# The branch gates of a hybrid decoder layer: from eight block products to seven, two of them beside the attention's tail

## The chip, the cores and the metric

The kernel runs on one core of one Trainium2 chip. The metric is the device time of one execution in microseconds. Three executions of the kernel before took 2147.61, 2152.07 and 2151.1 us, median 2151.1 us. A profile of one further execution stands beside them.

The core has five engines with a queue each, which work through their own queue in order and wait for one another by semaphores: TensorE (PE in the profile, with PEld for the loads of its stationary operand), VectorE (DVE), ScalarE (ACT), GpSimd (POOL) and SyncE (SP), which here issues every DMA. Tiles lie in SBUF, with 128 partitions; TensorE writes to PSUM, of which this kernel uses eight banks of 128 x 512 float32.

## The reference

One layer over 1024 tokens with a model width of 2048, in float32:

```python
h = rmsnorm(x, g_pre)
u = h @ w_in
gq, gk, gv, g_gate, g_lr, sq, sk, sv, s_gate = split(u)
o_gla = gla_chunked(gq, gk, gv, log_sigmoid(g_lr @ w_a2 + b_a) / 16)   # 4 heads
o_gla = rmsnorm(o_gla, g_gla_head) * silu(g_gate)
o_sb = stick_breaking(sq, sk, sv) * silu(s_gate)                       # 8 heads
mix = concat(o_gla, o_sb) @ w_out
h = x + rmsnorm(mix, g_post)
out = h + sigmoid(h @ w_ple_gate + b_ple_gate) * (p @ w_ple_proj)
```

The change concerns `g_gate` and `s_gate`, the two branch gates. Each is 1024 columns of `w_in`, so together they are one product of the 1024 x 2048 matrix `h` with a 2048 x 2048 matrix, followed by silu and a multiplication with the attention's output.

## The kernel before

**Layout.** Everything is kept transposed: a tile has 128 features in its partitions and 512 tokens (one half of the sequence, `hf` 0 or 1) in its free dimension. The input `x`, times `g_pre`, lies in `x_act[hf][k]` for the whole projection, 16 blocks of 128 features for each half. The factor of the RMSNorm, `rstd[hf]`, is applied to a result, not to the input.

**Precision.** A float32 operand is held as two tiles, a rounded high part (ScalarE, L104) and the rest as a low part (VectorE, L105). A block product is then three matmuls of 128 x 128 by 128 x 512 into one PSUM bank: high by high, low by high, high by low (L94 is the helper that records every matmul).

**Weights.** There are two kinds of weight tiles. `wload` (L112) brings 128 x 512 (`raw`, `hi`, `lo`) from a pool `w`. `wload2` and `wsplit` (L764, L769) bring 128 x 1024 (`wr` with four buffers, `wh` and `wl` with three) from a pool `mix`, which is opened after the projection has ended. `ar` (three buffers) stages other 128 x 1024 tiles from DRAM in the later part.

**Stages.** `dense` (L135) computes one unit, 128 output columns for both halves, over 16 blocks: 96 matmuls. Units 0 to 39 are the heads' keys, queries and values. Beside them runs the attention: generators in a queue `jobs`, of which `step()` (L156), called once in each of the 16 blocks, advances one at a set rate. So the order of the work is written out by hand as a sequence, with matmuls of the projection and pieces of the attention interleaved. A scheduler at compile time then orders each engine's instructions by this sequence, by raised priorities (`high_priority`: weight loads 700 ahead, evacuations 300 ahead) and by when its own model has their operands and tile buffers ready. A tile's buffer comes back when its last reader is done.

Units 40 to 55 are the branch gates. The first four (`early_gate`, L684) run while the attention still works on its last head; their 128 x 512 tiles come from the attention's ring `u` of twelve buffers. The next ten (`evac_gate`, L702) follow in a pool `gates`. A gate's evacuation multiplies the result with `rstd`, takes a sigmoid, multiplies with the attention's output read back from `o_d`, and stores to `og_d`. The last two units ("late solo", L891 to L917) run in the pool `mix` with wide tiles, one half after the other, beside jobs that read `og_d` back and form sums.

After that the kernel multiplies with `w_out` and with `w_ple_gate`. Both of these 1024 x 2048 by 2048 x 2048 products are already made of seven block products instead of eight (the Strassen-Winograd form): `A11`, `A12`, `A22` and the combinations `S1` to `S4` on one side, and weight blocks combined to `T1` to `T4` on the other. `product` (L777) is one of them for 128 output columns and 512 tokens: 8 blocks, 24 matmuls. `t2_d` and `t3_d` hold combined weights in DRAM for later stages, `fill` (L803) makes a set of eight operands from DRAM, and `st_u` and `st_v` (`u(j)`, `v(j)`) hold running sums in the buffers of the first half's `x_act`.

The PSUM banks are four for results (`dn`), two for `z`, and one each for `t` and `o`.

## Time and profile before

| quantity | value |
|---|---|
| median of three executions | 2151.1 us |
| profiled execution | 2153.95 us, span from first to last instruction 2151.8 us |
| TensorE busy | 2115.5 us, 98% of the span, 9904 matmuls |
| VectorE busy | 1374.1 us, 64% |
| ScalarE busy | 831.0 us, 39% |
| DMA | 300.38 MB, 140 GB/s over the span |

"Busy" is the union of the times in which an engine had an instruction in hand. Matmuls overlap, so the time that a matmul adds is their spacing. In the rows by line, "out<-in" names the tiles written and read, then come the shape, the count, the total and mean time, and the idle time just before with what ended it. In rows of stretches stand each engine's busy time and instruction count, the clock granted to TensorE as a share of full speed, the share of time the DMA engines were busy, and the bytes they moved. The share over the whole span hides that stages differ: DMA moves 54 to 120 GB/s during the attention and 176 to 329 GB/s in the slices behind the wide gates, up to the last but one.

### The profile page before, as it was taken

The page shows a single profiled execution, that of the slowest core. Times are in us where ns is not written, and L with a number is a line of the kernel's source. Part 1 is how long each engine was busy: PE and PEld are TensorE (multiplying, and loading weights), DVE is VectorE, ACT ScalarE, POOL GpSimd, SP SyncE. Part 2 cuts the span into 40 slices and gives each one's busy share as a digit, 9 for nine tenths or more (in the row PEclk, how much of TensorE's full clock was granted, in tenths as well). Part 3 has the DMA queues.
Part 4 walks back from the last instruction along what each step waited for, and adds up shares of the span by engine and source line. Part 5 has one row for each costly group of instructions (what it writes and reads, how often), then busy time and mean ns, then how long its engine had stood idle before and what let it go on. Part 6 is the DMA issues. An engine that isn't in the chain of part 4 may idle for free.

```text
span 2151.8 us, 26865 instructions
## 1 busy us (share of the span) xinstructions
PE 2115.5 (98%) x9904; PEld 1747.3 (81%) x9904; DVE 1374.1 (64%) x2147; ACT 831.0 (39%) x1347; POOL 106.4 (5%) x228
## 2 busy tenths in 40 slices
PE   9999999999999999999999999979999999999998
PEld 6788888888888888888888888868788888778887
DVE  8557676766666666666666232336687787885665
ACT  7333333333455454544544111123233344322332
POOL 3000000000101110110110000000000000000000
PEclk9999999999999999999999999989999999999999
DMA  6222222222233333333344333258787686786763
GB/s 205 73 54 56 59 61 59 55 59 58 62 86 86 75 85 91 85 85 76 93 101 120 93 98 98 87 176 314 291 329 255 207 302 210 265 289 225 232 206 122
DMA packets 215843, 300.38 MB, mean 140 GB/s; under 512 B 122912, under 2 KB 127904, under 8 KB 215712
## 3 DMA queue, kind: packets, MB, share of 16 engines
q1 hardware_dynamic: 215712, 298.67, 45.0%
q8 instruction: 77, 1.26, 0.2%
q14 instruction: 54, 0.44, 0.1%
HBM read 215.25 MB, written 56.10 MB: 126 GB/s over the span
## 4 chain that ended last, share of the span: by engine, by line
PE 82%; DMA 8%; DVE 6%; issue 2%; ACT 1%; SPq 1%; DVEq 0%; ACTq 0%
PE dn L94 72%; PE z L94 6%; PE t L94 2%; PE o L94 2%; DMA wr<-w_g 2%; DVE wl L105 1%; DMA ar<-og_d 1%; DMA xraw<-xT 1%; DMA ar<-h_d 1%; DVE al L105 1%; DMA wr<-w_out 1%; DMA ar<-c_d 0%; DMA ar<-xT 0%; DMA t_d<-wr 0%; DVE wr L759 0%
## 5 line engine op out<-in xcount | busy, mean ns | idle before, releaser
L94 PE MATMUL dn<-ah,hi 128*128 128x512 f32 x1728 | 686.9, 397 | 0.2 <-ACT u L666 0.2
L94 PE MATMUL dn<-al,hi 128*128 128x512 f32 x1728 | 675.4, 391 | 0.9 <-DVE al L230 0.9
L94 PE MATMUL dn<-ah,lo 128*128 128x512 f32 x1728 | 674.3, 390 | 0.0
L94 PE MATMUL dn<-ah,wh 128*128 128x512 f32 x960 | 375.4, 391 | 11.2 <-ACT wh L104 11.2
L94 PEld LDWEIGHTS dn<-al,hi 128*128 128x128 f32 x1728 | 324.3, 188 | 73.0 <-DVE al L230 2.3
L94 PEld LDWEIGHTS dn<-ah,hi 128*128 128x128 f32 x1728 | 324.8, 188 | 72.2 <-issue 2.8
L94 PE MATMUL dn<-ah,wl 128*128 128x512 f32 x960 | 375.7, 392 | 4.6 <-DVE wl L105 4.6
L94 PE MATMUL dn<-al,wh 128*128 128x512 f32 x960 | 374.5, 390 | 0.5 <-DVE al L105 0.5
L94 PEld LDWEIGHTS dn<-ah,lo 128*128 128x128 f32 x1728 | 325.0, 188 | 61.1
L104 ACT ACTIVATE hi<-raw 128x512 fp32r<-128x512 f32 x216 | 135.5, 628 | 300.6 <-PE dn L94 298.7
L105 DVE TENSOR_TENSOR lo<-raw,hi 128x512 fp32r<-128x512 f32 x216 | 150.3, 697 | 151.1 <-ACT hi L104 150.5
L94 PEld LDWEIGHTS dn<-ah,wh 128*128 128x128 f32 x960 | 181.3, 189 | 49.7 <-ACT wh L104 11.6
L94 PEld LDWEIGHTS dn<-ah,wl 128*128 128x128 f32 x960 | 181.6, 189 | 43.3 <-DVE wl L105 5.5
L94 PEld LDWEIGHTS dn<-al,wh 128*128 128x128 f32 x960 | 181.2, 189 | 38.6 <-DVE al L105 1.0
L104 ACT ACTIVATE wh<-wr 128x1024 fp32r<-128x1024 f32 x120 | 126.1, 1056 | 200.0 <-PE dn L94 125.3
L105 DVE TENSOR_TENSOR wl<-wr,wh 128x1024 fp32r<-128x1024 f32 x120 | 146.0, 1219 | 23.4 <-ACT wh L104 22.6
L309 ACT ACTIVATE X<-E 128x256 uint16<-128x256 uint16 (+2 forms) x96 | 81.0, 844 | 136.2 <-DVE E L582 123.2
L577 DVE TENSOR_TENSOR_SCAN X<-X 128x128 f32<-128x128 f32 (+2 forms) x96 | 98.3, 1024 | 36.8 <-POOL X L571 24.4
L592 DVE COPY v<-E 128x512 uint16<-128x512 uint16 (+1 forms) x160 | 63.6, 429 | 67.1 <-DMA E<-X 58.0
L104 ACT ACTIVATE ah<-ar 128x1024 fp32r<-128x1024 f32 x48 | 50.9, 1061 | 100.6 <-DVE ar L762 48.5
L105 DVE TENSOR_TENSOR s<-v,s 128x512 fp32r<-128x512 f32 (+1 forms) x82 | 52.2, 637 | 46.5 <-ACT s L104 46.0
L104 ACT ACTIVATE s<-v 128x512 fp32r<-128x512 f32 (+1 forms) x82 | 47.9, 584 | 76.8 <-DVE v L592 48.7
(208 smaller groups left out, 2181.3 us busy)
## 6 DMA issues: line engine op xcount, KB each, us to landing
raw<-w_in SPq DMA_DIRECT2D x216, 256.0 KB, 2.7
wr<-w_g SPq DMA_DIRECT2D x64, 512.0 KB, 4.3
wr<-w_out SPq DMA_DIRECT2D x56, 512.0 KB, 4.6
ar<-og_d SPq DMA_DIRECT2D x36, 512.0 KB, 5.3
ar<-h_d SPq DMA_DIRECT2D x36, 512.0 KB, 4.8
xraw<-xT SPq DMA_DIRECT2D x32, 256.0 KB, 4.4
o_d<-o SPq DMA_DIRECT2D x32, 256.0 KB, 2.1
t_d<-wr SPq DMA_DIRECT2D x16, 512.0 KB, 3.7
```

The source lines that it names most:

```text
L94: PE.matmul(o, lhsT, rhs, start=start, stop=stop)
L104: A.activation(hi, src, AF.Copy)
L105: (eng or V).tensor_tensor(lo, src, f(hi), op=ALU.subtract)
L309: A.activation(pl.rearrange("p (two n) -> p two n", two=2), src.bitcast(U16)[:, :2 * n].rearrange("p (n two) -> p two n", two=2), AF.Copy)
L577: V.tensor_tensor_scan(rev, rev, rev, initial=kq[:, n:n + 1], op0=ALU.mult, op1=ALU.bypass)
L592: V.tensor_copy(to[:, :, :m, j], w[:, :, 2 * g:2 * g + m])
```

## The change

The gates' product is made of seven block products too. With the two halves of the tokens as rows of blocks and the two halves of the features as columns of blocks, `A11` is `x_act[0][:8]`, `A12` is `x_act[0][8:]`, and `A22` is `x_act[1][8:]`. The gates' weights are a new input, `w_gate`, laid out as `w_out` is.

- `small_product` computes one block product for 128 columns with the narrow weight tiles: 24 matmuls, and a `step()` at every second block. Eight of them make `A11` by `B11`, kept in DRAM (`u1_d`). Eight make `A12` by `B21`; their evacuation (`gate_11`) adds `u1_d` and finishes the gates of the first 1024 columns for the first half. Fourteen run where the four early gates ran; the last two (`LAST_11`) come after the attention's pools have been closed.
- A third queue, `beside`, is advanced in every `step()`. Its generators make `S2` (with the sums kept in `sx_d`) and `S1` from `x`, read again from DRAM through `u` tiles, and put them where `x_act[1][:8]` and `x_act[0][:8]` were.
- Then come the wide stages: `S2` and `S1` with combined weights (16 products), `A22` (8), `S3` (8, each result finishing two gates of the second half) and `S4` (8, the remaining gates of the first half). `gate` finishes a pair of units on a 128 x 1024 tile. The sums for the out projection are queued one row at a time in the `S4` stage.
- The pool `w` moves to the right-hand side of SBUF. `mix` is opened before `w` is closed and stays open, with the tags `wr`, `wh`, `wl` and `ar` alone; the other tags lie in a pool `late` on the right, opened when `w` is closed.
- The order of two slots for operand sets is exchanged.

```diff
--- before.py
+++ after.py
@@ -40,15 +40,9 @@
-    offs += [OFF_GG + P * n for n in range(8)]
-    offs += [OFF_SG + P * n for n in range(8)]
-N_UNITS = len(unit_offsets())
-GATE0 = 40
-EARLY_GATES = 4
-LATE_SOLO = 2
...
+LAST_11 = 2
...
-    w_open = tc.tile_pool(name="w", bufs=4)
+    w_open = tc.tile_pool(name="w", bufs=4, side="right")
...
-    urgent, jobs = deque(), deque()
+    urgent, jobs, beside = deque(), deque(), deque()
...
     def step():
         advance(urgent)
+        advance(beside)
         rate[0] += rate[1]
...
-        def early_gate(n):
-            def go(hf, p):
-                gu, ol = at("u"), at("u")
-                dma2(ol, part(o_d[hf][n // 2], n))
-                V.tensor_tensor(gu, p, rstd[hf], op=ALU.mult)
+        u1_d = [dram.tile([P, W], F32, name=f"u1_d{i}") for i in range(4)]
+        sx_d = [dram.tile([P, W], F32, name=f"sx_d{i}") for i in range(4)]
+        g_sets = {"S1": [], "S2": []}
...
+        def x_part(hf, k):
+            t = at("u")
+            dma2(t, part(xT[hf, k // 2], k))
+            return t
+        def x_sum(k):
+            t, a = x_part(1, k + 8), x_part(1, k)
+            A.activation(t, t, AF.Copy, scale=g_of(k + 8))
+            V.scalar_tensor_tensor(t, a, g_of(k), t, op0=ALU.mult, op1=ALU.add)
+            return t
+        def x_set(name, hf, k, t, wides={}):
+            if k % 2 == 0:
+                wides[name] = act_wide(hf, k // 2)
+            pair = tuple(part(x, k) for x in wides[name])
+            split(*pair, t)
+            g_sets[name].append(pair)
+        def x_sets_2():
+            for k in range(8):
+                t, c = x_sum(k), x_part(0, k)
+                yield 1
+                V.scalar_tensor_tensor(c, c, g_of(k), t, op0=ALU.mult, op1=ALU.subtract)
+                dma2(part(sx_d[k // 2], k), c)
+                yield 1
+                x_set("S2", 1, k, c)
+                yield 1
+        def x_sets_1():
+            for k in range(8):
+                t = x_sum(k)
+                yield 1
+                x_set("S1", 0, k, t)
+                yield 1
+        def small_product(a, src, evac):
+            p = ps("dn")
+            for q in range(2):
+                hi, lo = wload(part(src, q))
+                for kk in range(4):
+                    k = 4 * q + kk
+                    sl = slice(kk * P, (kk + 1) * P)
+                    ah, al = a[k]
+                    mm(p, hi[:, sl], ah, k == 0, False)
+                    mm(p, lo[:, sl], ah, False, False)
+                    mm(p, hi[:, sl], al, False, k == 7)
+                    if k % 2:
+                        step()
+            with tc.high_priority(offset=300):
+                evac(p)
+        def keep_u1(j):
+            def go(p):
+                t = at("u")
+                A.activation(t, p, AF.Copy)
+                dma2(part(u1_d[j // 2], j), t)
+            return go
+        def gate_11(j, new):
+            def go(p):
+                gu, ol = new(), new()
+                dma2(gu, part(u1_d[j // 2], j))
+                dma2(ol, part(o_d[0][j // 2], j))
+                V.tensor_tensor(gu, p, gu, op=ALU.add)
+                V.tensor_tensor(gu, gu, rstd[0], op=ALU.mult)
                 V.tensor_tensor(ol, ol, gu, op=ALU.mult)
                 A.activation(gu, gu, AF.Sigmoid)
                 V.tensor_tensor(ol, ol, gu, op=ALU.mult)
-                dma2(part(og_d[hf][n // 2], n), ol)
+                dma2(part(og_d[0][j // 2], j), ol)
             return go
-        for n in range(EARLY_GATES):
-            dense(U(GATE0 + n), x_act, HALVES, early_gate(n))
-        while urgent or jobs:
+        beside.append(x_sets_2())
+        for j in range(8):
+            small_product(x_act[0][:8], w_gate[0, 0, j], keep_u1(j))
+        beside.append(x_sets_1())
+        for j in range(8 - LAST_11):
+            small_product(x_act[0][8:], w_gate[1, 0, j], gate_11(j, lambda: at("u")))
+        while urgent or jobs or beside:
+            advance(beside)
             advance(urgent) or advance(jobs)
         own[0].__exit__(None, None, None)
-    with tc.tile_pool(name="gates", bufs=1, reuse_waits="tile") as gp:
-        def evac_gate(n):
-            def go(hf, p):
-                gu = gp.tile([P, HT], F32, tag="gu", name=nm("gu"), bufs=2)
-                gs = gp.tile([P, HT], F32, tag="gs", name=nm("gs"), bufs=1)
-                ol = gp.tile([P, HT], F32, tag="ol", name=nm("ol"), bufs=2)
-                dma2(ol, part(o_d[hf][n // 2], n))
-                V.tensor_tensor(gu, p, rstd[hf], op=ALU.mult)
-                A.activation(gs, gu, AF.Sigmoid)
-                V.tensor_tensor(ol, ol, gu, op=ALU.mult)
-                o = gp.tile([P, HT], F32, tag="oB", name=nm("oB"), bufs=1)
-                V.tensor_tensor(o, gs, ol, op=ALU.mult)
-                dma2(part(og_d[hf][n // 2], n), o)
-            return go
-        for n in range(EARLY_GATES, KT - LATE_SOLO):
-            dense(U(GATE0 + n), x_act, HALVES, evac_gate(n))
+    mp = ctx.enter_context(tc.tile_pool(name="mix", bufs=1, reuse_waits="tile"))
+    late = [None]
+    def mt(tag, bufs, n=W, dt=F32, name=None):
+        pool = mp if tag in ("wr", "wh", "wl", "ar") else late[0]
+        return pool.tile([P, n], dt, tag=tag, name=nm(name or tag), bufs=bufs)
+    for j in range(8 - LAST_11, 8):
+        small_product(x_act[0][8:], w_gate[1, 0, j], gate_11(j, lambda: part(mt("ar", 3), 0)))
     w_open.__exit__(None, None, None)
-    slots = [[(1, kp) for kp in range(4)], [(1, kp) for kp in range(4, 8)], [(0, kp) for kp in range(4)]]
-    with tc.tile_pool(name="mix", bufs=1, reuse_waits="tile") as mp:
-        def mt(tag, bufs, n=W, dt=F32, name=None):
...
+    late[0] = ctx.enter_context(tc.tile_pool(name="late", bufs=1, reuse_waits="tile", side="right"))
+    if True:
+        slots = [[(1, kp) for kp in range(4, 8)], [(1, kp) for kp in range(4)], [(0, kp) for kp in range(4)]]
...
+        wide = {}
+        def gate(n, hf, p, other):
+            key = n // 8, hf
+            if n % 2 == 0:
+                wide[key] = mt("ev", 2)
+            z = wide[key]
+            with soon():
+                add(part(z, n), p, other)
+            if n % 2 == 0:
+                return
+            o, g = staged(o_d[hf][n // 2]), mt("sq", 1)
+            z3 = z.rearrange("p (a t) -> p a t", a=2)
+            V.tensor_tensor(z3, z3, rstd[hf].rearrange("p (o t) -> p o t", o=1).to_broadcast([P, 2, HT]),
+                            op=ALU.mult)
+            A.activation(g, z, AF.Sigmoid)
+            V.tensor_tensor(z, z, o, op=ALU.mult)
+            V.tensor_tensor(z, z, g, op=ALU.mult)
+            dma2(og_d[hf][n // 2], z)
...
+        def make_x3(i):
+            a, b = staged(xT[1, i]), staged(xT[0, i])
+            times_g(b, i)
+            return g_then(a, i, b, ALU.subtract)
+        def make_x4(i):
+            a, b = staged(xT[0, i + 4]), staged(sx_d[i])
+            return g_then(a, i + 4, b, ALU.add)
+        t2_d, t3_d = drams("g2_d", 8), drams("g3_d", 8)
+        for i in range(4):
+            dma2(st_u[i], u1_d[i])
+        for j in range(8):
+            with ahead():
+                b11, t1, t2 = (wload2(w_gate[kh, nh, j]) for kh, nh in ((0, 0), (0, 1), (1, 1)))
+                sub(t1, t1, b11)
+                sub(t2, t1, t2)
+                w2, w1 = wsplit(t2), wsplit(t1)
+                add(b11, b11, t2)
+                dma(t2_d[j], t2)
+                dma(t3_d[j], b11)
+            p = product(g_sets["S2"], w2)
+            with soon():
+                add(u(j), p, u(j))
+            p = product(g_sets["S1"], w1)
+            with soon():
+                add(v(j), p, u(j))
+        drain()
+        job(fill("S3", 1, make_x3))
+        job(fill("S4", 2, make_x4))
+        for j in range(8):
+            with ahead():
+                t4, t2 = wload2(w_gate[1, 0, j]), wload2(t2_d[j])
+                add(t4, t4, t2)
+                w = wsplit(t4)
+            p = product(x_act[1][8:], w)
+            with soon():
+                add(u(j), p, u(j))
+        drain()
+        for j in range(8):
+            with ahead():
+                w = wsplit(wload2(t3_d[j]))
+            p = product(sets["S3"], w)
+            gate(j, 1, p, u(j))
+            gate(8 + j, 1, p, v(j))
+        drain()
         early = []
-        for hf in (1, 0):
-            if hf == 0:
-                job(fill("A11", 0, plain(og_d[1])))
-                job(sums_12(range(3), None, early))
-            for n in range(KT - LATE_SOLO, KT):
-                p = None
-                for kh in HALVES:
-                    with ahead():
-                        raw = mt("wr", 4)
-                        for q in range(2):
-                            dma(part(raw, q), w_in[GATE0 + n, 2 * kh + q])
-                        w = wsplit(raw)
-                    p = product(x_act[hf][8 * kh:8 * kh + 8], w, p=p, last=kh == 1)
-                with soon():
-                    if n % 2 == 0:
-                        z = mt("ev", 2)
-                    V.tensor_tensor(part(z, n), p, rstd[hf], op=ALU.mult)
-                    if n % 2:
-                        o, g = staged(o_d[hf][n // 2]), mt("sq", 1)
-                        A.activation(g, z, AF.Sigmoid)
-                        V.tensor_tensor(z, z, o, op=ALU.mult)
-                        V.tensor_tensor(z, z, g, op=ALU.mult)
-                        dma2(og_d[hf][n // 2], z)
+        job(fill("A11", 0, plain(og_d[1])))
+        for j in range(8):
+            with ahead():
+                w = wsplit(wload2(w_gate[1, 1, j]))
+            p = product(sets["S4"], w)
+            gate(8 + j, 0, p, v(j))
+            if j in (1, 3, 5):
+                job(sums_12((j // 2,), None, early))
         drain()
+        st_u, st_v = state("h"), state("l")
...
+        "w_gate": quarters(np.concatenate([w[:, OFF_GG:OFF_GG + D // 2], w[:, OFF_SG:OFF_SG + D // 2]], axis=1)),
```

More of the change, by code (lines that the diff above doesn't have):

```diff
@@ L60, with layer @@
 RATE_BG = 0.5
+LAST_11 = 2
 @with_exitstack
-def layer(ctx, tc, xT, w_in, w_lr, w_a2, b_a, g_pre, g_head, w_out, g_post,
+def layer(ctx, tc, xT, w_in, w_gate, w_lr, w_a2, b_a, g_pre, g_head, w_out, g_post,
           w_g, b_g, w_p, pT, ident, masks, sel_in, out):
@@ L775, in layer, with product @@
         soon = functools.partial(tc.high_priority, offset=300)
-        def product(a, w, mid=None, at=4, p=None, last=True):
-            first = p is None
-            p = p or ps("dn")
+        def product(a, w, mid=None, at=4):
+            p = ps("dn")
             hi, lo = w
@@ L783, in product @@
                 ah, al = a[k]
-                mm(p, hi[:, sl], ah, first and k == 0, False)
+                mm(p, hi[:, sl], ah, k == 0, False)
                 mm(p, lo[:, sl], ah, False, False)
-                mm(p, hi[:, sl], al, False, last and k == 7)
+                mm(p, hi[:, sl], al, False, k == 7)
                 if mid and k == at:
@@ L1009, in layer @@
         drain()
-        p_act, pw, res, wide = {}, {}, {}, {}
+        p_act, pw, res = {}, {}, {}
         def load_p(hf):
```

13 lines of the change are left out of this document (9 added, 4 removed).

## The prediction

> **What bounds the kernel now.** I read the page's share of busy time first, then its chain of work that ended last, then its groups of instructions.
>
> ```profile
> span 2151.8 us, 26865 instructions
> PE 2115.5 (98%) x9904; PEld 1747.3 (81%) x9904; DVE 1374.1 (64%) x2147; ACT 831.0 (39%) x1347; POOL 106.4 (5%) x228
> PE 82%; DMA 8%; DVE 6%; issue 2%; ACT 1%; SPq 1%; DVEq 0%; ACTq 0%
> L94 PE MATMUL dn<-ah,hi 128*128 128x512 f32 x1728 | 686.9, 397 | 0.2 <-ACT u L666 0.2
> L94 PE MATMUL dn<-ah,wh 128*128 128x512 f32 x960 | 375.4, 391 | 11.2 <-ACT wh L104 11.2
> ```
>
> TensorE is the bound, so a removed matmul is worth its spacing, not its 391 ns: those overlap. The spacing comes from the chain in order of time.
>
> ```profile
> 1187.88 226.50 PE dn L94 x999
> ...
> 1419.69 0.70 DVE oB L712
> 1420.41 0.32 SPq L713
> ...
> 1421.26 3.79 DMA wr<-w_in
> ...
> 1425.15 1.06 ACT wh L104
> ...
> 1427.52 7.01 PE dn L94 x23
> ...
> 1508.01 5.41 DMA t_d<-wr
> ...
> 1525.66 5.71 DMA wr<-w_out
> ```
>
> 226.50 / 999 = 0.2267 us for one matmul of 512 columns. The same chain shows the hole ahead of the late solo gates: the last product of the wide gates has ended, a result is multiplied and stored, and only then is the first wide weight tile loaded and rounded. Next, busy time in stretches (columns: stretch, PE, PEld, DVE, ACT, POOL busy with counts, granted clock, DMA share, GB/s).
>
> ```profile
> 70.00:1097.00 1027.00, 1024.89 (x5093) 858.07 (x5092) 667.36 (x1308) 445.20 (x831) 75.04 (x184) 1.00 0.29 71
> 1097.00:1197.00 100.00, 100.00 (x482) 84.11 (x481) 59.68 (x110) 43.53 (x83) 8.71 (x24) 1.00 0.42 116
> 1197.00:1415.00 218.00, 218.00 (x962) 180.20 (x961) 64.17 (x98) 35.02 (x57) 0.00 (x0) 1.00 0.29 91
> 1415.00:1435.00 20.00, 8.31 (x28) 6.35 (x28) 6.94 (x9) 4.88 (x6) 0.00 (x0) 0.66 0.66 212
> 1471.00:1520.00 49.00, 49.00 (x218) 40.59 (x217) 28.98 (x25) 17.80 (x21) 0.00 (x0) 1.00 0.86 311
> 1520.00:1540.00 20.00, 15.34 (x56) 11.54 (x55) 12.24 (x11) 4.73 (x5) 0.00 (x0) 0.83 0.86 305
> 1540.00:1610.00 70.00, 70.00 (x310) 58.00 (x309) 56.47 (x56) 22.81 (x22) 0.00 (x0) 1.00 0.84 313
> ```
>
> The gates run from 1097 to about 1474. Their first 318 us have no hole and leave VectorE and DMA half idle. In 1415 to 1435 there are 28 matmuls, worth 28 × 0.2267 = 6.35 us, so 13.65 us are lost, part of it at a granted clock of 0.66. In 1520 to 1540 (56 matmuls, 12.7 us) another 7.3 us are lost, where a store and a reload of weights delay the out projection's first combined products.
>
> **Matmuls removed.** The gates take 16 units × 2 halves × 16 blocks × 3 = 1536 matmuls; seven products of 8 × 8 × 3 = 192 make 1344. 192 × 0.2267 = **43.5 us less**, on the engine that sets the end. The sums are made of these elementwise prices:
>
> ```profile
> L105 DVE TENSOR_TENSOR lo<-raw,hi 128x512 fp32r<-128x512 f32 x216 | 150.3, 697 | 151.1 <-ACT hi L104 150.5
> L105 DVE TENSOR_TENSOR wl<-wr,wh 128x1024 fp32r<-128x1024 f32 x120 | 146.0, 1219 | 23.4 <-ACT wh L104 22.6 <-DMA ar<-xT 0.4
> L759 DVE TENSOR_TENSOR st<-dn,st 128x512 f32<-128x512 f32 x64 | 43.9, 685 | 25.1 <-PE dn L94 25.1
> L759 DVE TENSOR_TENSOR wr<-wr,wr 128x1024 f32<-128x1024 f32 x32 | 39.2, 1225 | 43.6 <-DMA wr<-w_g 33.3 <-DMA wr<-t_d 10.1
> L884 DVE SCALAR_TENSOR_TENSOR ar<-ar,c,rstd 128x512 f32<-128x512 f32 x16 | 11.6, 748 | 8.1 <-DMA ar<-c_d 8.1
> L104 ACT ACTIVATE wh<-wr 128x1024 fp32r<-128x1024 f32 x120 | 126.1, 1056 | 200.0 <-PE dn L94 125.3 <-DVE wr L762 34.8 <-issue 27.6
> ```
>
> The Trainium skill ("TensorE: Matmul & The Clock Gate", section "Back-to-back issue gap") gives about 131 ns per 512-column matmul in a sustained stream, by which the saving would be an estimated 25 us and the time some 18 us later than mine. The row of 999 matmuls says 227 ns here, and the measurement decides.
>
> **The old hole.** Its 13.65 us go, since the wide tiles no longer wait for the gates pool's last store. What stands in its place is costed next.
>
> **Beside the attention's tail.** The four early gates (384 matmuls) become fourteen small products (336). The stretch from 1097 to 1197 holds 384 × 0.2267 = 87.0 us of gates and 13 us of attention, so the new one asks 336 × 0.2267 + 13 = 89 us of TensorE. Attention's pace per matmul is kept: a step comes every six matmuls in both. Before, the steps reach the attention's last values about 57 steps in; now 56 steps are laid and the rest is drained at once, with two more products behind.
>
> ```profile
> L619 SPq DMA_DIRECT2D o_d<-o x16: 326/327/580, 611.5 to 1188.6; - x16
> L687 SPq DMA_DIRECT2D u<-o_d x8: 354/432/612, 1107.5 to 1193.8; - x8
> ```
>
> Its last output is stored at 1188.6, so it still ends with the sixth product. VectorE: of its 59.7 us, the early gates' 16 low parts (11.2) and the 18 operations of six evacuations (at 0.685, 12.3) go, leaving 36 for the attention. Added: 28 low parts (19.5), the difference sets (8 × (2 × 0.75 + 0.70) = 17.6), the sum sets (8 × 1.45 = 11.6) and six gate evacuations of four (16.4). That is 101 us of work in 89. The excess of 12 us either is deferred (gate evacuations can wait behind four PSUM banks) or stalls TensorE: bounds 0 and 12.
>
> **Entry into the combined weights.** The first difference needs three 512 KB tiles, two subtractions and a rounding: from the DMA rows below 4.3, then 1.2 + 1.2 + 1.1 = 8 us, under the cover of two small products, 48 × 0.2267 = 10.9 us. But the tiles lie where the attention's tiles were, and a slot that the sixth gate's evacuation used comes free only after its four operations, its sigmoid and its 2 us store, itself behind the 12 us excess: then the load starts up to 15 us after the sixth product and 12 us are uncovered. The second weight block is tight as well: with four raw tiles it waits for the first's store (3.7), a reload (4.3) and two subtractions, as at 1520, where 7.3 us were lost. Bounds for tail and entry together 2 and 31; I take **15**, nearest to the old hole's 13.65, because the same kind of wait rules it.
>
> ```profile
> raw<-w_in SPq DMA_DIRECT2D x216, 256.0 KB, 2.7
> wr<-w_g SPq DMA_DIRECT2D x64, 512.0 KB, 4.3
> ...
> t_d<-wr SPq DMA_DIRECT2D x16, 512.0 KB, 3.7
> ...
> og_d<-oB SPq DMA_DIRECT2D x20, 256.0 KB, 2.0
> ```
>
> **The combined stage** (384 matmuls, 87 us) asks of VectorE per block three weight sums (3.7), two low parts (2.4) and two evacuations (1.4): 7.5 of 10.9 us, and 23 MB, 265 GB/s. The stretch 1540 to 1610 carries the same pattern at a full TensorE: 0 here.
>
> **The A22 stage** (192 matmuls, 43.5 us): eight blocks of 1 MB of weights and two set fills of 4.2 MB make 16.8 MB, 386 GB/s; the fastest stretch without a stall moved 311 GB/s, so the bytes ask 54 us, 10.4 more. Only half of the fills is needed by the next stage, and three staging tiles slow them down, so bounds 0 and 10, taken **3**.
>
> **The last two gate stages.** In the S3 stage each product feeds two gates. Per pair of blocks (10.9 us): two low parts (2.4), four evacuations (2.7), six wide multiplications (7.3): 12.5 us of VectorE. A result tile also returns only after its store: last evacuation, multiplications, the one sigmoid tile's turn and 3.7 us of store give about 14 us a pair. Four pairs run 4 × 3.1 = 12 us late, of which the four PSUM banks hide some 11. The S4 stage asks 29.9 + 4 fills of 1.2 + 11 for three rows of sums = 46 of 43.5, and 18.4 MB. Bounds 0 and 19, taken **5**. Behind it the first out-projection stage has VectorE time to recover, and the loss at 1520 stays: its causes are not touched (−6 to +8, taken 0).
>
> The Trainium skill ("DMA: Bandwidth & Descriptors", section "Where 436 GB/s comes from") puts the HBM limit of one core at about 358 GB/s; by it the A22 stage's bytes would take an estimated 47 us and its upper bound would be 3.5 us instead of 10. The stretch at 311 GB/s ran at a DMA share of 0.86, which fits that limit, but no row shows it sustained, so the sum goes by 311.
>
> **Sum:** −43.5 − 13.65 + 15 + 3 + 5 = −34.2 us. The profiled execution took 2153.95 us, 2.15 more than its span; 2153.95 − 34.2 = 2119.8. The median of the runs shown is 2.85 lower, so I predict **2117 us**; with ±13 for my middle values, 2104 to 2130.
>
> **Rivals.**
> 1. *VectorE and DMA bind the last stages.* The lag in the A22, S3 and S4 stages is passed on whole: 10.4 + 12.4 + 6.5 (S4's 2.3 and four sigmoids of 1.06) = 29 in place of 8, so 2138 (2130 to 2147). For it: 12.5 of 10.9 us. Against: low parts and evacuations come ahead of the multiplications by priority, and PSUM holds four products.
> 2. *Clean.* The scheduler defers the excess and the first weights are in time: only 2 us lost, 2096 (up to 2104). For it: the whole stretch 70 to 1097 loses 2 us. Against: VectorE never had over 100% to do there.
> 3. *Slower, by the attention's twelve `u` tiles.* Sixty helper tiles pass through them beside the last head, which holds seven or eight until its end. At a load of 2.7 us, two operations and a store or a split, a helper stays about 6.5 us: 390 tile-us in 4.5 × 89 = 400. If VectorE's queue makes that 12.5 us, 750 / 4.5 = 167 us are asked: 78 over, less 10.9 of cover, plus 8 behind = 75 against 57 won, +18: 2169. It decides from about 11 us a tile. For it: sum and difference sets sit behind the attention's work at over 100%. Against: the list is laid out by readiness, and a helper's own work is short.
> 4. *No net gain:* the stalls come to 57 us and eat both terms, 2151. It needs every upper bound (31 + 10 + 19) at once.
>
> **Chances:** forecast 0.54, first rival 0.20, clean 0.09, no net gain 0.06, slower 0.11. About 0.2% (4.3 us) is what a measurement of this kernel can tell from no change. Faster 0.83, same 0.06, slower 0.11. The range 2098 to 2146 leaves out the slower case, the unchanged one and a third of the clean one: 0.20.
>
> **What would show it.** 192 matmuls fewer, 2624 groups of three in place of 2688 over `dn`, still near 0.227 us apart. A hole of some 5 to 15 us ahead of the first `wh` of the gates, released by a DMA into `wr` or a subtraction there. VectorE at 95% or more from 1097 to 1190. In the S3 stage VectorE above 90% with TensorE idle for under 10 us. It is wrong if the attention's last store comes later than about 1200, if TensorE is idle over 20 us in the S3 and S4 stages, or if the combined stage runs below full speed past its first two blocks.

## The result, and the profile after

The changed kernel takes **2164.59 us** (median of four, 2163.33 to 2170.56), the kernel before 2150.12 us beside it (four, 2147.61 to 2152.07): a ratio of 1.0073, 95% interval [1.0051, 1.0095]. It is **slower by 0.73%**, where I had forecast 2117 us and had put slower at 0.11. The profiled execution is the slowest of these four, 6 us above their median, so losses read from it can be some 6 us too large in sum. The page of the changed kernel, with the lines that answer to those of before (span, busy time, DMA, the high-part matmuls with narrow and with wide weights):

```profile
span 2168.7 us, 26868 instructions
PE 2104.2 (97%) x9712; PEld 1716.6 (79%) x9712; DVE 1509.6 (70%) x2275; ACT 882.5 (41%) x1401; POOL 110.3 (5%) x228
...
DMA packets 229669, 354.92 MB, mean 164 GB/s; under 512 B 124448, under 2 KB 129440, under 8 KB 229536
...
L89 PE MATMUL dn<-ah,hi 128*128 128x512 f32 x1408 | 569.1, 404 | 0.2 <-ACT u L662 0.2
...
L89 PE MATMUL dn<-ah,wh 128*128 128x512 f32 x1216 | 478.1, 393 | 32.6 <-ACT ah L99 19.4
```

The 192 matmuls are gone (9904 to 9712, and 1408 + 1216 = 2624 groups of three). But TensorE's busy time fell by 11.3 us only, not by 43.5, and its time without work rose from 2151.8 - 2115.5 = 36.3 to 64.5 us, where my sum had it rise to 36.3 - 13.65 + 23 = 45.7. One matmul with narrow weights went from 397 to 404 ns in hand; with wide ones it is 393 against 391. DMA moves 54.5 MB more. In stretches (columns as before: stretch, PE, PEld, DVE, ACT, POOL busy, granted clock, DMA share, GB/s):

```profile
70.00:1097.00 1027.00, 1025.82 (x5017) 845.14 (x5016) 663.08 (x1298) 443.18 (x827) 76.49 (x184) 1.00 0.29 72
1116.00:1216.00 100.00, 91.84 (x420) 74.32 (x419) 81.39 (x145) 66.14 (x125) 9.81 (x24) 0.97 0.92 264
1220.00:1245.00 25.00, 10.48 (x37) 7.46 (x35) 11.59 (x17) 4.45 (x7) 0.00 (x0) 0.76 0.67 243
1245.00:1430.00 185.00, 185.00 (x806) 152.96 (x806) 146.27 (x154) 56.46 (x60) 0.00 (x0) 0.99 0.81 283
1425.00:1475.00 50.00, 48.65 (x215) 39.99 (x214) 40.62 (x40) 18.93 (x19) 0.00 (x0) 1.00 0.77 265
1500.00:1550.00 50.00, 29.40 (x106) 21.39 (x104) 26.50 (x23) 11.87 (x13) 0.00 (x0) 0.80 0.87 310
```

Four things are to be seen. From 70 to 1097, where the change neither adds nor removes work, TensorE is as full as before and runs 76 matmuls fewer (5093 before). Beside the attention's tail, DMA is busy 0.92 of the time (0.42 before). From 1220 to 1245 there is a hole ahead of the combined weights. The gate stages that I had feared (1245 to 1475) are full but for 1.4 us. And from 1500 to 1550, at the entry of the out projection's combined stage, 106 matmuls run, worth 24.0 us: 26.0 us are lost, against 7.3 before. Two milestones, the last value of the projection and the last store of the attention (columns: count, then duration in ns, first and last start in us):

```profile
L615 SPq DMA_DIRECT2D o_d<-o x16: 326/327/579, 621.0 to 1228.6; - x16
L295 DVE TENSOR_TENSOR v<-dn,rstd x32: 683/692/693, 91.9 to 1115.3; 128x512 f32<-128x512 f32 x32
```

The same row of the kernel before ends at 1099.2, and its attention's last store was at 1188.6:

```profile
L299 DVE TENSOR_TENSOR v<-dn,rstd x32: 675/692/693, 90.2 to 1099.2; 128x512 f32<-128x512 f32 x32
```

So the projection ends 16.1 us later, the attention's tail takes 113.3 us in place of 89.4, and the chain of waits shows the two holes:

```profile
1227.25 15.38 issue
1242.63 2.01 ACT wh L99 x2
...
1244.69 15.40 PE dn L89 x55
```

```profile
1526.20 1.24 DVE wr L813
1527.82 4.92 DMA ar<-o_d
1532.76 1.24 DVE ev L959
...
1535.16 1.23 DVE al L100
...
1536.43 11.54 PE dn L89 x40
```

The first hole's 15.38 us "issue" hide a load: in SyncE's queue the loads of the first wide weights are issued only after the attention's last store. Their tiles lie where the attention's tiles were.

```profile
1228.61 0.38 SPq L615 DMA_DIRECT2D o_d<-o  x1
...
1232.01 2.84 SPq L820 DMA_DIRECT2D wr<-w_gate  x4
```

The second hole ends on the split of a sum (`al`, L100) at 1535.2. Ahead of it stands the last of the branch gates: in SyncE's queue its `o` tile is loaded at 1527.8, after weight stores, with the loads of the stored sums behind it, and in VectorE's queue its multiplications (L959, L960) come before the split.

So there are three places to explain: the projection (+16), the tail with its hole, and the entry at 1500.

### The profile page after: what moved, and what is told of

The parts are those of the page before. It is cut to its first block, busy times and chain, and to the rows that moved or that the text cites. A ratio compares the mean times of both kernels' runs of the same rounds, so it can differ in the third digit from the quotient of the medians.

```text
span 2168.7 us, 26868 instructions
## 1 busy us (share of the span) xinstructions
PE 2104.2 (97%) x9712; PEld 1716.6 (79%) x9712; DVE 1509.6 (70%) x2275; ACT 882.5 (41%) x1401; POOL 110.3 (5%) x228
## 4 chain that ended last, share of the span: by engine, by line
PE 72%; DMA 13%; DVE 9%; issue 4%; ACT 2%; SPq 1%; DVEq 0%; POOL 0%; ACTq 0%
PE dn L89 63%; PE z L89 5%; DMA wr<-w_g 3%; PE t L89 2%; PE o L89 2%; DVE wl L100 2%; DMA u<-xT 1%; DMA E<-X 1%; DVE ev L813 1%; DMA ar<-og_d 1%; DMA og_d<-ev 1%; DMA xraw<-xT 1%; DMA ar<-xT 1%; DMA ar<-h_d 1%; DMA wr<-w_out 1%
## 5 line engine op out<-in xcount | busy, mean ns | idle before, releaser
L89 PE MATMUL dn<-ah,hi 128*128 128x512 f32 x1408 | 569.1, 404 | 0.2 <-ACT u L662 0.2
L89 PE MATMUL dn<-al,hi 128*128 128x512 f32 x1408 | 557.8, 396 | 0.3 <-DVE al L226 0.3
L89 PE MATMUL dn<-ah,lo 128*128 128x512 f32 x1408 | 557.8, 396 | 0.0
L89 PE MATMUL dn<-ah,wh 128*128 128x512 f32 x1216 | 478.1, 393 | 32.6 <-ACT ah L99 19.4
L89 PE MATMUL dn<-ah,wl 128*128 128x512 f32 x1216 | 476.7, 392 | 0.0
L89 PE MATMUL dn<-al,wh 128*128 128x512 f32 x1216 | 476.3, 392 | 0.1
L89 PEld LDWEIGHTS dn<-ah,hi 128*128 128x128 f32 x1408 | 265.8, 189 | 65.5 <-issue 2.8
L89 PEld LDWEIGHTS dn<-al,hi 128*128 128x128 f32 x1408 | 265.3, 188 | 65.4 <-DVE al L226 1.2
L89 PEld LDWEIGHTS dn<-ah,lo 128*128 128x128 f32 x1408 | 266.1, 189 | 54.3
L100 DVE TENSOR_TENSOR wl<-wr,wh 128x1024 fp32r<-128x1024 f32 x152 | 184.5, 1219 | 11.7 <-ACT wh L99 11.4
L100 DVE TENSOR_TENSOR lo<-raw,hi 128x512 fp32r<-128x512 f32 x192 | 133.7, 698 | 58.6 <-ACT hi L99 58.2
L816 DVE TENSOR_TENSOR wr<-wr,wr 128x1024 f32<-128x1024 f32 x48 | 58.7, 1223 | 50.6 <-DMA wr<-w_gate 23.9
L813 DVE TENSOR_TENSOR wr<-wr,wr 128x1024 f32<-128x1024 f32 x48 | 58.8, 1224 | 48.0 <-DMA wr<-w_g 31.0
```

The source lines that it names most:

```text
L89: PE.matmul(o, lhsT, rhs, start=start, stop=stop)
L100: (eng or V).tensor_tensor(lo, src, f(hi), op=ALU.subtract)
L813: V.tensor_tensor(dst, a, b, op=ALU.add)
L816: V.tensor_tensor(dst, a, b, op=ALU.subtract)
```

## The experiments

They were measured on three occasions, on which the kernel before took 2152.77, 2152.99 and 2149.64 us; beside the changed kernel it had taken 2150.12. So a difference between medians of two occasions is uncertain by about 3 us. Ratios are to the kernel before on the same occasion; by them, what the experiments 2 and 5 to 9 gain on the changed kernel is 3 to 5 us more than by the medians.

**1. Is it the place of the weights' pool?** The kernel before, with this edit alone:

```diff
-    w_open = tc.tile_pool(name="w", bufs=4)
+    w_open = tc.tile_pool(name="w", bufs=4, side="right")
```

> The kernel before, with one line changed: the pool of the narrow weight tiles lies on the right-hand side of SBUF, as in the changed kernel. Theory 'place': the narrow matmuls' spacing, 228.9 ns before and 233.9 ns after, follows the place of the narrow weight tiles alone. Then this kernel's 5184 narrow matmuls go from 229 to 234 ns and it takes 5184 x 5.0 ns = 26 us more than the kernel before, about 2176. Rival 'surroundings': the slower spacing in the changed kernel comes from something else (its other tiles' places, its order of instructions): then this one is within 5 us of the kernel before, spacing 229 ns.

Measured: 2175.24 us (2175.06 to 2176.84) against 2152.77, ratio 1.0103 [1.0087, 1.0120]. The same stretch of this kernel:

```profile
70.00:1097.00 1027.00, 1026.86 (x5022) 845.88 (x5021) 662.58 (x1297) 442.03 (x826) 75.94 (x184) 1.00 0.29 71
```

The loss is there without the rest of the change. From successive starts in the trace, a narrow matmul follows its forerunner after 233.8 ns on average (228.9 in the kernel before), a wide one after 226.8 (226.7). 5184 narrow ones by 4.9 ns make 25 us; 22.5 were measured.

**2. Address or region?** In the changed kernel an unused tile of 64 bytes lies at the right end, so that `hi` and `lo` start 64 bytes lower.

```diff
+    pad = ctx.enter_context(tc.tile_pool(name="pad", bufs=1, side="right"))
+    nc.vector.memset(pad.tile([P, 16], F32, name="pad_t"), 0.0)
     w_open = tc.tile_pool(name="w", bufs=4, side="right")
```

> The changed kernel, with an unused tile of 64 bytes a partition at the right-hand end of SBUF, so that the narrow weight tiles start 64 bytes lower: at the same remainder by 512 (416) as the operands in x_act and as the wide weight tiles, where they had 480. Theory 'alignment': the spacing depends on where within 512 bytes a weight tile starts; then the narrow spacing falls from 233.9 to about 229 ns and the kernel gains 4224 x 5.0 ns = 21 us, about 2143. Rival 'region': the upper end of SBUF is slower as such; then nothing changes, 2164 and 234 ns.

Measured: 2152.92 us (2148.87 to 2160.76), ratio to before 1.0003 [0.9990, 1.0016]; narrow spacing 229.5 ns.

```profile
70.00:1097.00 1027.00, 1024.39 (x5080) 857.19 (x5079) 668.28 (x1309) 446.70 (x832) 75.51 (x184) 1.00 0.30 72
```

64 bytes give back nearly all of the spacing, and 11.7 us of the time by the medians (15 by the ratios) where 21 were expected; the region is cleared. The projection now ends at 1101.5, 14 us earlier.

**3. Own address or distance?** All left-hand tiles are shifted by 64 bytes, the narrow weights stay.

```diff
     ones_r = const.tile([P, P], F32R, name="ones_r")
+    nc.vector.memset(const.tile([P, 16], F32, name="pad_t"), 0.0)
```

> The changed kernel with an unused 64-byte tile among the constants at the left end of SBUF: activations start at remainder 1504 of 2048 bytes instead of 1440, wide weights too, and the narrow weights keep their 2016. Output unchanged. Theory 'own start': the matmul spacing goes by the remainder of the weights' own address (2016 slow, 1440 fast; 96 of 128 against 32 of 128): narrow products stay at 234 ns and wide ones (1504, 96 of 128) become 232 to 234 ns too, which adds some 25 to 33 us: 2185 to 2200. Rival 'distance': what counts is the distance from the weights to the activations, slow where it is no multiple of 512 bytes; then narrow ones (2016 - 1504 = 512) are 229 ns, wide ones (0) 227 ns: 2148 to 2157.

Measured: 2150.2 us in one execution; narrow 229.5 ns, wide 226.7.

```profile
70.00:1097.00 1027.00, 1025.58 (x5096) 858.31 (x5095) 669.93 (x1312) 447.25 (x835) 74.85 (x184) 1.00 0.30 73
```

The weights' own address is not it: 2016 of 2048 is fast here, and wide weights at 1504 stay fast. The distance to the left-hand tiles counts.

**4. Which distance?** The pad of the second experiment with 192 bytes (`[P, 48]`).

> The changed kernel with an unused tile of 192 bytes at the right end of SBUF: the narrow weights start at remainder 1824 of 2048 bytes, 384 = 3 x 128 above the activations' 1440; output unchanged. So far the distance 576 is slow (234 ns) and 0, 512 and 1024 are fast (227 to 229.5 ns). If only the remainder by 128 counts (576 is 64, 384 is 0): 229 to 230 ns and 2149 to 2157 us. If the distance has to be a multiple of 512: 233 to 235 ns and 2161 to 2168 us.

Measured: 2162.22 us in one execution, narrow spacing 233.0 ns.

```profile
70.00:1097.00 1027.00, 1025.20 (x5027) 849.30 (x5026) 664.44 (x1298) 443.04 (x826) 76.01 (x184) 1.00 0.29 72
```

A multiple of 128 is not enough. All that was seen, by the compiled programs' addresses (remainders of 2048 bytes) and the traces' starts:

| kernel | weights | activations | distance, remainder by 512 | spacing, ns |
|---|---|---|---|---|
| before, narrow | 1440 | 1440 | 0 | 228.9 |
| before, wide | 416 | 1440 | 0 | 226.7 |
| before with `w` on the right, narrow | 2016 | 1440 | 64 | 233.8 |
| after, narrow | 2016 | 1440 | 64 | 233.9 |
| after, wide | 1440 | 1440 | 0 | 226.9 |
| 64 bytes lower, narrow | 1952 | 1440 | 0 | 229.5 |
| left side 64 higher, narrow | 2016 | 1504 | 0 | 229.5 |
| 192 bytes lower, narrow | 1824 | 1440 | 384 | 233.0 |

**5. The gate's operand first.** For the second hole: the load of `o` gets the weights' priority.

```diff
-            o, g = staged(o_d[hf][n // 2]), mt("sq", 1)
+            with ahead():
+                o = staged(o_d[hf][n // 2])
+            g = mt("sq", 1)
```

> The changed kernel, with the loads of the attention's output in the wide gates given the priority of the weight loads, ahead of the staging loads that the out projection's sums ask of the same three buffers. Theory 'staging order': the 26 us lost from 1500 to 1550 (7 before) come from gates of the S4 stage that wait for a staging buffer behind the sums, so that the last sums and the sets S1 and S2 are late; then the last gate's store moves from 1535 to about 1500, the hole shrinks to some 7 to 10 us and the kernel gains 15 to 19 us, about 2147. Rival 'bytes': the stretch is bound by the transfers as such (0.8 to 1.0 of the DMA's time): then at most 5 us are gained.

Measured: 2167.24 us (2164.19 to 2169.49), ratio 1.0063 [1.0048, 1.0078]. The last gate is stored 11 us earlier, at 1524.1, but the hole stays (102 matmuls from 1500 to 1550), and the 15 to 19 us of the theory don't come. Its chain of waits names what is late next:

```profile
1531.60 0.32 SPq L1058
...
1531.96 4.80 DMA ar<-s_d
1536.79 1.07 ACT ah L99
...
1537.89 1.22 PE dn L89 x2
```

A sum that had been stored is loaded back, behind a store of combined weights in SyncE's queue. So two reasons were to be told apart: the trip through DRAM, and the place in the queue.

**6. No trip through DRAM.** `gate` returns its tile, and the sums take it; the last row comes first in `last_sums`.

```diff
-                a, b, c = staged(og_d[0][i]), staged(og_d[0][i + 4]), staged(og_d[1][i])
+                a, b, c = staged(og_d[0][i]), z, staged(og_d[1][i])
```

> The changed kernel, but the sum of gated outputs takes its last operand (branch gate output of the last gate pair) from SBUF where the gate leaves it, without the store to DRAM and the load back, and the last row of the sums comes ahead of the three rows that are loaded back. Output unchanged. Theory 'round trip': the 26 us hole at the entry of the out projection's combined stage (1500 to 1550) is the trip of the last gate through DRAM; then the first combined product starts 10 to 16 us earlier, and the median is 2149 to 2155. Rival 'queue': the loads of the last rows stand in SyncE's queue behind weight loads that wait for a raw weight buffer, so taking one load out leaves the hole: 2160 to 2167, and the last matmul wait in that stage is again over 20 us and ends on the split of a sum.

**7. The loads first.** The edit of experiment 5, and the same priority for the loads of the sums' rows and of the stored sums.

```diff
-                a, b, c = staged(og_d[0][i]), staged(og_d[0][i + 4]), staged(og_d[1][i])
+                with ahead():
+                    a, b, c = staged(og_d[0][i]), staged(og_d[0][i + 4]), staged(og_d[1][i])
...
-                s1.append(to_slot(2, i, staged(s1_d[i])))
+                with ahead():
+                    t = staged(s1_d[i])
+                s1.append(to_slot(2, i, t))
```

> The changed kernel, but the loads of the gates' attention outputs and of the sums' rows are put on SyncE's queue ahead of weight loads (the same planner priority as the weights have), and nothing else. Output unchanged. Theory 'queue': the hole of 26 us shrinks by 10 to 19 us and the median is 2146 to 2155. Rival 'round trip': the store of the last gated output and its load back still follow each other, so the hole stays at 20 us or more: 2160 to 2168.

Measured: the sixth 2158.54 us (2154.21 to 2166.02), ratio 1.0027 [1.0015, 1.0039]; the seventh 2163.18 us (2160.63 to 2165.80), 1.0048 [1.0031, 1.0065]. The sixth lies between its two theories' numbers; the seventh lies in the range of its rival, "round trip". From 1500 to 1550 the sixth runs 143 matmuls (17.6 us lost by 0.2267 each) and the seventh 121 (22.6 us lost), against 106 in the changed kernel. Without the trip, what ends the hole is the place in the queue:

```profile
1520.25 0.33 SPq L1057
...
1520.63 4.96 DMA ar<-s_d
1525.61 1.06 ACT ah L99
```

With the loads first, it is the trip (store of the gate, load of it, subtraction):

```profile
1529.19 0.32 SPq L1061
...
1529.56 3.97 DMA og_d<-ev
1533.55 0.32 SPq L802
...
1533.97 5.79 DMA ar<-og_d
...
1539.85 1.24 DVE ar L816
```

So two late arrivals stand one behind the other; taking either away uncovers the other.

**8. Both, with the 64 bytes.** The diffs of experiments 2, 5, 6 and 7 together, the combination from here on.

> The changed kernel with the narrow weight tiles 64 bytes lower, the last gated output taken from SBUF, and the loads of the sums and gates ahead of the weights. Output unchanged. If the two losses (matmul spacing by the weight tiles' place, and the hole at the out projection's combined stage) are separate, this is 2153 less 10 to 19 us: 2134 to 2143, faster than both kernels, with the stage's loss under 12 us. If the hole only moves (the weights are then late in its place), 2149 to 2156.

Measured: **2132.61 us** (2128.84 to 2136.33) against 2152.99, ratio **0.9906 [0.9889, 0.9923]**; 20.3 us under the kernel with the 64 bytes alone, a little more than I had expected.

```profile
1500.00:1550.00 50.00, 50.00 (x222) 41.41 (x221) 40.52 (x38) 13.77 (x14) 0.00 (x0) 1.00 0.92 338
```

```profile
L617 SPq DMA_DIRECT2D o_d<-o x16: 326/327/580, 614.3 to 1212.7; - x16
L297 DVE TENSOR_TENSOR v<-dn,rstd x32: 675/691/693, 92.9 to 1102.0; 128x512 f32<-128x512 f32 x32
```

222 matmuls in 50 us: the second hole is gone altogether, and this version beats both kernels. TensorE is full there at 338 GB/s, so the bytes as such, the rival of experiment 5, were not what held it at 310. That the two losses were separate fits the sum; the edits of experiments 5 to 7 together, without the 64 bytes, were not run. The tail (1102.0 to 1212.7) is what is left.

**9. The tail without loads of `x`.** In the changed kernel, GpSimd zeroes a tile in place of each of the 40 loads.

```diff
             t = at("u")
-            dma2(t, part(xT[hf, k // 2], k))
+            G.memset(t, 0.0)
```

> The changed kernel without the 40 loads of x beside the attention's tail (10.5 MB): GpSimd fills the tiles with zeros instead; what ScalarE and VectorE do with them stays. So the gates' sets S1 and S2 and what follows from them hold no data of x. Theory 'DMA in the tail': the tail is bound by transfers (DMA share 0.9 to 1.0 from 1130 to 1220), so the attention ends some 15 to 25 us earlier and the kernel gains as much, about 2140 to 2149. Rival 'VectorE in the tail', the reason given in the prediction: its work is what is too long, so this gains under 6 us, 2158 or more.

Measured: 2155.28 us (2150.81 to 2158.24), ratio 1.0006 [0.9995, 1.0017]: 9.3 us under the changed kernel, between the two theories. The tail is 101.4 us (1115.9 to 1217.3) in place of 113.3.

```profile
1116.00:1216.00 100.00, 94.37 (x435) 77.25 (x434) 90.22 (x161) 68.44 (x129) 30.25 (x61) 0.97 0.65 187
```

VectorE, 81% busy there before, is now at 90%. A tile of the ring `u` is also held for a shorter time without its load, so the transfers and the ring aren't told apart.

**10. The tail without the sums too.** On the combination: no loads of `x`, no scaling, no `scalar_tensor_tensor`; the splits stay. Beside the diff of experiment 9:

```diff
-            t, a = x_part(1, k + 8), x_part(1, k)
-            A.activation(t, t, AF.Copy, scale=g_of(k + 8))
-            V.scalar_tensor_tensor(t, a, g_of(k), t, op0=ALU.mult, op1=ALU.add)
-            return t
+            return x_part(1, k)
...
-                t, c = x_sum(k), x_part(0, k)
+                c = x_part(0, k)
                 yield 1
-                V.scalar_tensor_tensor(c, c, g_of(k), t, op0=ALU.mult, op1=ALU.subtract)
```

> The combination (narrow weights 64 bytes lower, last gated output from SBUF, loads first), but the activation sums of the branch gate's combined products are left out altogether: no loads of x, no scaling on ScalarE, no scalar_tensor_tensor on VectorE; a tile zeroed on GpSimd is split in their place, 16 times as before, so the output isn't the reference's. With the attention's last store at 1212.7 and the projection's end at 1102.0 in the combination, the stretch between them is 110.7 us against 89.4 in the kernel before. Theory 'shared': the loads alone were worth 11 us in an earlier run, and VectorE's 22 operations of 0.75 us there (16 us) and ScalarE's 15 of 0.72 us are worth as much again, so the stretch falls to 88 to 96 us and the time by 12 to 22 us to 2110 to 2121. Rival 'loads only': VectorE's work fits beside the rest, the stretch is 98 to 102 us and the time 2119 to 2124. Rival 'products': it is the two times eight small products with their splits and gates that make the stretch long; then it stays above 102 us.

Measured: 2110.24 us in one execution, 22.4 us under the combination, or 19.0 when each is taken against the kernel before beside it.

```profile
L617 SPq DMA_DIRECT2D o_d<-o x16: 326/329/579, 612.4 to 1193.8; - x16
L297 DVE TENSOR_TENSOR v<-dn,rstd x32: 679/692/693, 90.6 to 1102.4; 128x512 f32<-128x512 f32 x32
```

The tail is 91.4 us, within 2 us of the 89.4 before the change, as the theory "shared" had it. So the small products with their gates fit beside the attention; the sums of `x`, loads and elementwise work together, are what doesn't. Since 16 tiles are taken from the ring `u` here in place of 40, the work of VectorE and ScalarE and the ring's tiles aren't told apart.

**11 and 12. Two attempts at the rest.** On the combination, four small products behind the tail (`LAST_11 = 4`), and with that the sum of the two scaled halves formed once, stored, and loaded back.

```diff
-LAST_11 = 2
+LAST_11 = 4
...
                 t, c = x_sum(k), x_part(0, k)
+                dma2(part(t_d[k // 2], k), t)
...
-                t = x_sum(k)
+                t = at("u")
+                dma2(t, part(t_d[k // 2], k))
```

> The combination, but four in place of two of the second set of small products run after the attention's tail, from the staging tiles (LAST_11 = 4). Output unchanged. Theory 'cover': the hole at the entry of the combined weights (TensorE idle some 14 us between 1210 and 1228, as the first wide loads wait until the tail's tiles are free) is covered by 11 us more of products, which in turn leave the tail: the attention's last store comes 3 to 8 us earlier and the time falls by 6 to 12 us to 2120 to 2127. Rival 'moves': the loads of the wide weights stand behind the loads of the four products in SyncE's queue, so the hole follows the products and the time is within 4 us of the combination, 2129 to 2136.

> As the run with four products after the tail, but the sum of two scaled halves of x, which is formed twice (once for each combined set), is formed once, stored and loaded back: the same bytes (8 stores and 8 loads in place of 16 loads), 8 operations fewer on VectorE and 8 on ScalarE. Output unchanged. Theory 'shared': 6 us of VectorE's work leave a stretch in which it is 80 to 95% busy, so the attention ends 2 to 6 us earlier and the time is 2 to 6 us under the run with four. Rival 'DMA': the stretch is held by the transfers, whose bytes are the same: within 2 us of the run with four, or above it, because a load of a sum now waits for its store.

Measured: 2135.15 us (2130.73 to 2137.67), ratio 0.9925 [0.9908, 0.9941], and **2127.15 us** (2125.38 to 2129.95), ratio **0.9895 [0.9881, 0.9910]**. With four products the attention ends 5.6 us earlier (1207.1), but the hole moves behind them; the chain of waits of that kernel has a gate's operand and a running sum in the queue behind the weights' stores:

```profile
1239.71 0.32 SPq L1001
...
1240.08 0.02 SPq L755
...
1240.13 3.69 DMA ar<-u_d
...
1251.81 4.60 DMA st<-u_d
...
1256.44 0.70 DVE st L815
```

So "moves" holds for the time. Forming the sum once doesn't shorten the tail (1099.4 to 1208.8, 109.4 us, against 105.8 with four products alone); its 8 us, more than either of its theories said, come behind the tail, as the same stretch of the two kernels shows (four products first, then with the sum formed once):

```profile
1230.00:1250.00 20.00, 13.94 (x54) 10.95 (x53) 13.80 (x15) 3.15 (x4) 0.00 (x0) 0.83 0.88 293
```

```profile
1230.00:1250.00 20.00, 20.00 (x90) 16.57 (x89) 18.29 (x22) 5.51 (x6) 0.00 (x0) 1.00 0.91 311
```

Why the queue falls out better there was not tested. Its interval overlaps the combination's: that it beats both kernels is shown, that it beats the combination isn't.

## Why the prediction was wrong

| TensorE, us | before | forecast | after | 64 bytes lower | combination |
|---|---|---|---|---|---|
| busy | 2115.5 | 2072 | 2104.2 | 2082.9 | 2081.5 |
| not busy | 36.3 | 45.7 | 64.5 | 66.8 | 48.3 |

Three steps failed: the place of the pool `w`, which was in no term; the loss at 1520, taken at 0; and the attention's tail, which was sized by VectorE's work without the transfers of `x`. One by one:

- **"192 x 0.2267 = 43.5 us less": right in count, and eaten elsewhere.** The first failed step isn't in the working: the pool `w` going to the right-hand side, which the diff shows and which I costed at nothing by leaving it out. TensorE's busy time is 32 us above the forecast; with 64 bytes of padding 21 of them go. Of the median, the place costs 11.7 us in the changed kernel and 22.5 in the kernel before, which has 5184 narrow matmuls against 4224 and a full TensorE behind them. Of the other 10.9 us, the traces account for 8.3 by stretches in which the granted clock was 0.50, most of them in or behind holes. Over all of these, the kernel with the 64 bytes runs 67 matmuls in 29.3 us of busy time, 14.1 more than 67 x 0.2267; the kernel before runs 28 in 12.1, 5.8 more. The longest, from 1498.4 to 1525.7 of the former, holds 20 matmuls in 9.65 us. The narrow spacing that is left (229.5 against 228.9 ns) makes 2.5 us more.
- **The spacing itself.** I took 0.2267 us, and the wide products keep it (226.9 ns). The rule of the Trainium skill that I had weighed ("TensorE: Matmul & The Clock Gate", section "Back-to-back issue gap", about 131 ns) is met by these products in no run here: their mean spacings are 226.7 to 233.9 ns.
- **"Loss at 1520 stays: its causes are not touched (-6 to +8, taken 0)": wrong, and the largest stall.** It was 26.0 us against 7.3. What failed is the assumption that the causes stay as they were: the last gates of the first half are now the last products before the out projection, and the sums that this stage needs hang on them through a store, a load and a queue. The combination is 20.3 us faster without these waits. I looked at the weights' path there, since the old loss was on that path, and not at what had moved in front of it.
- **"Beside the attention's tail ... it still ends with the sixth product" and "101 us of work in 89": the place was right, the size and the reason in part wrong.** I asked VectorE alone, bounds 0 and 12, and expected it 95% busy; it is at 81% (81.39 us of 100). The tail is 23.9 us longer, as the loads of `x` share in it: the transfers of these 40 loads were in no term of the sum, and DMA is busy 0.92 of the time there. Without them the tail is 11.9 us shorter; without the sums too, 19.3 us shorter in the combination. The sign that I had named, an attention's last store later than about 1200, came (1228.6). This also delays the entry.
- **"Tail and entry 15, bounds 2 and 31".** From 1116 to 1245 the rows of stretches give 8.2 + 14.5 = 22.7 us without work (from 1216 to 1220 TensorE is full), inside the bounds and above the value taken. That the first wide load would wait for the attention's last tiles was named, and it came.
- **Old hole gone, A22 taken 3, last gate stages taken 5: too dear.** 1245 to 1430 is full, 1425 to 1475 loses 1.4 us. The first rival (VectorE and DMA bind there) is out: VectorE is at 81% in the latter. The 54 us of the A22 stage came from 311 GB/s as the fastest stretch without a stall. That reading was wrong already (the row from 1540 to 1610 has 313), and from 1330 to 1375 the changed kernel moves 324 GB/s at a full TensorE.
- **The slower rival named the right stretch, but not the sign's cause.** It asked for 75 us of stall from the ring `u` in the tail; the tail is 24 us longer, and no run shows the ring as the reason. What made the kernel slower is the sum of three losses (by the medians, place 11.7, entry of the out projection 20.3, sums of `x` 22.4), of which the forecast held 15 in all. The third isn't to be won back whole, since the kernel needs these sums. Without the first two the kernel is faster by 0.94%. That 2132.6 lies in the range given (2098 to 2146) is in part luck: the tail's term was too small and those of the gate stages too large.

## What to carry to other kernels

When a pool is moved, compare the matmuls of an untouched stretch between the two traces (count in the same microseconds) before looking for the loss in the edited stages: 76 matmuls fewer from 70 to 1097 named this one at once. When stages change their order, list for each stage the latest operand and the store, queue and load that bring it; taking away one of two late arrivals in a row shows little (6 and 1.4 us by the medians here, against 20.3 with both), so try both together. Count the loads that are put beside a stage, not only the engine's work.

## What the runs showed of the hardware

The distance in SBUF between the stationary weights and the left-hand tiles, the activations that stream against them among these, changes the mean spacing of the matmuls of 512 columns on rounded float32 tiles (fp32r in the rows): 226.7 to 229.5 ns in five cases where it is a multiple of 512 bytes, 233.0 to 233.9 ns in three where it isn't (64 or 384 bytes over). That is about 2%. All three slow cases are narrow tiles on the right-hand side; no wide tile was tried off a multiple of 512. It follows neither the weights' own start nor the region. What else moved with the left-hand tiles isn't separated, remainders other than 0, 64 and 384 were not tried, and the mechanism stays open. All these starts fulfil what the Trainium skill asks in "SBUF — State Buffer", section "Operand start alignment" (a multiple of the element's size), which it states as a matter of legality, not of speed.
